# Out projection of a hybrid decoder layer: the first two groups of output columns contract over seven row blocks, and over the eighth when both are through

## The chip, the cores and the metric

One core of a Trainium2 chip runs the whole program. The metric is the device time of one execution in microseconds (us); a kernel's time is the median of several runs. A profiled execution also has a span, from its first instruction to its last. The engines are called PE (TensorE, the matrix unit; PEld is its weight load), DVE (VectorE), ACT (ScalarE), POOL (GpSimd) and SP (SyncE, which issues most transfers).

## What is computed

A decoder layer over 512 tokens of width 1024 in float32. Two token mixers run side by side, a dilated attention and a state-space layer; their merged result passes the out projection and is added to the input; a SwiGLU network, a gated embedding and a norm follow.

```python
h = h + (gate_attn * attn_d + gate_ssm * ssm_d) @ w_out      # the out projection, 1024 x 1024
n2 = rmsnorm(h, g_ffn)
h = h + (silu(n2 @ w_ffn_gate) * (n2 @ w_ffn_up)) @ w_ffn_down
h = h + sigmoid(h @ w_ple_gate) * (p @ w_ple_proj)
return rmsnorm(h, g_final)
```

## The kernel before

Activations lie transposed: 128 features on the partitions, 512 tokens along the row, and a width of 1024 is eight such row blocks. Every float32 matrix product is made of three passes. An operand is split into a high part (rounded to the format that PE multiplies fast) and a low part (the rest), and `mm3` issues high x high (L407), high weights x low activations (L408) and low weights x high activations (L409) into one PSUM bank. `gemm` does this for each row block of the contraction, so one group of 128 output columns over eight row blocks is 24 matmuls of 512 columns.

The weights of a group come as one chunk of 128 x 1024. SP loads it into a `raw` buffer (four of them); ACT rounds it to `whi`; DVE subtracts to get `wlo` (three buffers of each, in turn). `gemm` asks for the split of the next chunks at its fourth row block (`ws.ahead(2)`). The high part is put on ACT's queue at once. The low part is deferred, and is put on DVE's queue when the program's own estimate of time says that `whi` is there:

```python
sca.copy(hi[:, :sz], t[:, :sz])
def low():
    dve.tensor_sub(lo[:, :sz], t[:, :sz], hi[:, :sz].bitcast(F32))
    while self.nd < min(i + 1 + RAW_BUFS, len(chunks)):
        self.dma()
defer(dve, low, hi)
```

The engines run their queues in the order in which this program is written and estimated; an instruction that waits holds everything behind it on its engine.

The merge loop ends with the eighth row block of the merged activation `mT`: DVE makes the sum `t1`, ACT rounds it into `mT[:, 0, 7]`, and DVE subtracts for the low part `mT[:, 1, 7]`. Then the out projection goes over its eight groups m = 0 to 7. For each: four transposes of the input on PE (L403) into an `aux` bank and a copy of it to `h1T` on ACT; 24 matmuls of `mT` with the chunk `wo` into an `mm` bank; an add of the bank to `h1T` on DVE (the add); a scaled rounding to `h1g` on ACT (the scaling); a `SCALAR_TENSOR_TENSOR` on DVE for the low part of `h1g`; and on POOL the square of `h1T` and its sum in `ssq`. `h1g` is what the SwiGLU network reads. The wrappers record every DVE, ACT and POOL operation at L167.

Of the kernel before, what the change touches and what calls it, by code (L numbers as in the profile page):

```python
# [20 lines left out]
KD = D // P  # L21
# [58 lines left out]
def kernel(  # L80
# [15 lines left out]
    def tile_name(ap):  # L96
        return getattr(ap, "tensor", ap).name
# [107 lines left out]
    def nm(s):  # L205
        uid[0] += 1
        return f"{s}_{uid[0]}"
# [4 lines left out]
    def bank(tag):  # L212
        name = nm(tag)
        used = banks[tag]
        if len(used) >= 4:
            bank_free[name] = last_read.get(used[-4], 0.0)
        used.append(name)
        return psum.tile([P, 512], F32, tag=tag, name=name, bufs=4)

    def mm_ps():  # L220
        return bank("mm")

    def aux_ps():
        return bank("aux")
# [13 lines left out]
    class Weights:  # L238
# [40 lines left out]
        def get(self, key, more=1):  # L279
            i = self.np  # L280
            self.np += 1
            assert keys[i] == key, (keys[i], key)
            self.ahead(more)
            wh, wl = self.hl.pop(i)
            if tile_name(wl) not in ready:
                flush(True)
            return wh, wl
# [61 lines left out]
    get = ws.get  # L349
# [7 lines left out]
    def flush(force=False):  # L357
        for item in list(held):
            eng, aps, fn = item
            if force or when(*aps) <= max(now(), eng.free):  # L360
                held.remove(item)
                fn()
# [9 lines left out]
    def tick(limit=3.0, kinds=KINDS, keys=()):  # L372
        flush()
        for item in [item for item in bg if item[2] in kinds]:
            while item[0] <= now() and dve.lag() < limit and sca.lag() < limit:
                if keys and done.issuperset(keys):
                    return
                try:
                    item[0] = next(item[1]) + now()
                except StopIteration:  # L380
                    bg.remove(item)
                    break
# [18 lines left out]
    def transpose(ps, src, n=P):  # L401
        pe_step(ps, 0.07, src)
        nc.tensor.transpose(ps, src, ident[:n, :n])  # L403

    def mm3(ps, lh, ll, rh, rl, start, stop):
        pe_step(ps, 3 * (0.0135 + 0.000417 * rh.free_size()), lh, ll, rh, rl)
        nc.tensor.matmul(ps, lhsT=lh, rhs=rh, start=start, stop=False)  # L407
        nc.tensor.matmul(ps, lhsT=lh, rhs=rl, start=False, stop=False)  # L408
        nc.tensor.matmul(ps, lhsT=ll, rhs=rh, start=False, stop=stop)  # L409

    def gemm(ps, w, c0, act, start=True, stop=True, k0=0):
        wh, wl = w
        ah, al = act
        nk = wh.shape[1]
        for k in range(nk):
            mm3(ps, wh[:, k, c0:c0 + P], wl[:, k, c0:c0 + P], ah[:, k0 + k, :], al[:, k0 + k, :],
                start and k == 0, stop and k == nk - 1)
            if k == 3:
                ws.ahead(2)
            if k < nk - 1:  # L420
                tick()
# [827 lines left out]
    ps = mm_ps()  # L1249
# [75 lines left out]
    ps = aux_ps()  # L1325
# [84 lines left out]
    mT = apool.tile([P, 2, KD, T], F32R, tag="A", name="mT")  # L1410
    flush(True)
    for mp in range(4):
# [10 lines left out]
        for j in range(2):  # L1423
            m = 2 * mp + j
# [25 lines left out]
    for r in range(4):  # L1450
        pt = L4.tile([P, PLE], F32, tag="pt", name=nm("pt"), bufs=4)
        pool.dma_start(pt, p_r[r])
        pts.append(pt)
    for m in range(KD):
        ps = aux_ps()
        for r in range(4):
            transpose(ps[:, r * P:(r + 1) * P], xr[:, r, m * P:(m + 1) * P])
        sca.copy(h1T[:, m], ps)
        ps = mm_ps()
        gemm(ps, get("wo"), 0, (mT[:, 0], mT[:, 1]))  # L1460
        dve.tensor_add(h1T[:, m], h1T[:, m], ps)
        sca.activation(h1g[:, 0, m], h1T[:, m], AF.Copy, scale=gffn[:, m:m + 1])
        dve.scalar_tensor_tensor(h1g[:, 1, m], h1T[:, m], gffn[:, m:m + 1],
                                       h1g[:, 0, m].bitcast(F32), op0=ALU.mult, op1=ALU.subtract)
        if m == 0:
            pool.tensor_mul(ssq, h1T[:, m], h1T[:, m])
        else:
            sq = L4.tile([P, T], F32, tag="sq", name=nm("sq"), bufs=2)
            pool.tensor_mul(sq, h1T[:, m], h1T[:, m])
            pool.tensor_add(ssq, ssq, sq)  # L1470
# [25 lines left out]
    for hf in range(2):  # L1496
        for f in range(NF):
# [16 lines left out]
            if hf == 1 and 3 <= f < 7:  # L1514
                r = f - 3
                ps = aux_ps()
# [6 lines left out]
        if hf == 1:  # L1523
            late = L4.tile([P, 2, 4, D], F32, tag="B", name="late")
            h3, proj = late[:, 0], late[:, 1]
            for c in range(2):
                wph, wpl = get("pp")
                cs = slice(512 * c, 512 * c + 512)
                for r in range(4):
                    sl = slice(r * P, (r + 1) * P)  # L1530
                    ps = aux_ps()
# [3 lines left out]
        for m in range(KD):  # L1535
            ps = mm_ps()
# [53 lines left out]
    for kh in range(4):  # L1590
        w = get("pg")
# [54 lines left out]
    for r in range(4):  # L1646
        for c0, n in ((512, 512),) if r < 3 else ((512, 256), (768, 256)):
            pt_ = aux_ps()[:, 0:n]
            back(pt_, c0 // P, n // P, r)
            ps = mm_ps()[:, 0:n]  # L1650
# [53 lines left out]
```

## Time and profile before

| what | value |
|---|---|
| time, median of 3 runs | 936.71 us (936.27 to 937.2) |
| the profiled execution's own time | 936.02 us |
| its span | 934.2 us |
| PE busy | 922.1 us, 99% of the span |
| DVE, ACT, POOL busy | 492.7, 354.4, 128.9 us |
| granted clock of PE, mean | 0.996 |

A granted clock of 1.00 is 2.4 GHz and 0.50 is 1.2 GHz. A start time in a row counts from the beginning of the span. A row's duration of a matmul is longer than its distance to the next, since they overlap; the distance is what it costs.

### The profile page before, as it was taken

What the parts mean: (1) busy time and instruction counts of PE and PEld (TensorE: products, weight loads), DVE (VectorE), ACT (ScalarE), POOL (GpSimd) and SP (SyncE); (2) the same over time, 40 slices, a digit from 0 to 9 for tenths busy, and PEclk for the clock granted to TensorE, in tenths of its full rate; (3) what the DMA queues carried; (4) which work ended last, traced back from release to release, by engine and by line L of the source; (5) the groups of instructions that cost most, each with busy time, mean ns of one, the idle gap of its engine ahead of it and who ended that gap; (6) DMA issues with size and microseconds to landing.
All of it is one profiled execution on the core that took longest, in us unless ns stands there. A gap on an engine that the chain in (4) does not pass through costs nothing.

```text
span 934.2 us, 11591 instructions
## 1 busy us (share of the span) xinstructions
PE 922.1 (99%) x4539; PEld 776.9 (83%) x4539; DVE 492.7 (53%) x795; ACT 354.4 (38%) x514; POOL 128.9 (14%) x211
## 2 busy tenths in 40 slices
PE   9999999999999999999999999999999999999995
PEld 8888888888988888888788888888888888888885
DVE  6973685577675573356655443432243443234536
ACT  5434555445453543322432322322223332332423
POOL 4117960000000000000143111110001111100021
PEclk9999999999999999999999999999999999999998
DMA  8629314225243542322333333223333333133402
GB/s 242 204 89 157 117 46 116 79 80 116 69 116 88 148 129 77 105 91 77 124 116 91 101 103 91 76 62 110 113 113 91 100 103 98 50 93 99 158 1 91
DMA packets 165103, 96.33 MB, mean 103 GB/s; under 512 B 19985, under 2 KB 158009, under 8 KB 164921
## 3 DMA queue, kind: packets, MB, share of 16 engines
q1 hardware_dynamic: 162936, 92.68, 35.5%
q10 hardware_dynamic: 1520, 1.64, 0.6%
q0 software_dynamic: 592, 1.28, 0.4%
q8 instruction: 35, 0.57, 0.2%
q14 instruction: 20, 0.16, 0.1%
HBM read 90.84 MB, written 4.75 MB: 102 GB/s over the span
## 4 chain that ended last, share of the span: by engine, by line
PE 95%; DVE 2%; DMA 1%; ACT 1%; issue 0%; SPq 0%; DVEq 0%; ACTq 0%
PE mm L408 22%; PE mm L409 22%; PE mm L407 22%; PE aux L399 6%; PE aux L409 6%; PE aux L407 6%; PE aux L408 6%; PE aux L403 2%; PE mm L1241 1%; DMA raw<-in_w_in_dram 1%; DVE t L167 1%; DVE wlo L167 0%; DVE fst L167 0%; ACT qk L167 0%; DVE pk L167 0%
## 5 line engine op out<-in xcount | busy, mean ns | idle before, releaser
L167 DVE TENSOR_TENSOR wlo<-raw,whi 128x1024 fp32r<-128x1024 f32 (+2 forms) x162 | 192.5, 1201 | 101.2 <-ACT whi L167 96.7
L167 ACT CAST whi<-raw 128x1024 fp32r<-128x1024 f32 (+2 forms) x162 | 160.7, 996 | 126.6 <-issue 57.7
L407 PE MATMUL mm<-xn,whi 128*128 128x512 f32 x352 | 139.3, 396 | 0.0
L409 PE MATMUL mm<-xn,wlo 128*128 128x512 f32 x352 | 137.2, 390 | 0.0
L408 PE MATMUL mm<-xn,whi 128*128 128x512 f32 x352 | 137.1, 390 | 0.0
L409 PEld LDWEIGHTS mm<-xn,wlo 128*128 128x128 f32 x352 | 66.1, 188 | 13.9
L407 PEld LDWEIGHTS mm<-xn,whi 128*128 128x128 f32 x352 | 66.2, 188 | 13.1 <-issue 0.2
L408 PEld LDWEIGHTS mm<-xn,whi 128*128 128x128 f32 x352 | 66.2, 188 | 12.9
L407 PE MATMUL mm<-h1g,whi 128*128 128x512 f32 x176 | 68.9, 392 | 0.0
L407 PE MATMUL aux<-h1g,whi 128*128 128x512 f32 x176 | 68.6, 390 | 0.0
L409 PE MATMUL mm<-h1g,wlo 128*128 128x512 f32 x176 | 68.5, 389 | 0.0
L408 PE MATMUL mm<-h1g,whi 128*128 128x512 f32 x176 | 68.5, 389 | 0.0
L409 PE MATMUL aux<-h1g,wlo 128*128 128x512 f32 x176 | 68.5, 389 | 0.0
L408 PE MATMUL aux<-h1g,whi 128*128 128x512 f32 x176 | 68.5, 389 | 0.0
L407 PE MATMUL mm<-act,whi 128*128 128x512 f32 x176 | 68.5, 389 | 0.0
L408 PE MATMUL mm<-act,whi 128*128 128x512 f32 x176 | 68.5, 389 | 0.0
L409 PE MATMUL mm<-act,wlo 128*128 128x512 f32 x176 | 68.5, 389 | 0.0
L167 POOL TENSOR_TENSOR tg<-tg,tu 128x512 f32<-128x512 f32 x22 | 28.4, 1291 | 271.9 <-DVE tu L167 260.5
L167 DVE TENSOR_TENSOR h1T<-h1T,mm 128x512 f32<-128x512 f32 x24 | 16.5, 688 | 78.8 <-PE mm L409 78.8
L167 ACT CAST act<-tg 128x512 fp32r<-128x512 f32 x22 | 13.7, 622 | 90.7 <-POOL tg L167 90.7
L1447 POOL DMA_DIRECT2D gfin<-in_g_final_dram x1 | 0.6, 629 | 331.1 <-DVE mT L167 331.1
L167 DVE TENSOR_TENSOR tu<-aux,rs 128x512 f32<-128x512 f32 x22 | 15.2, 691 | 57.4 <-PE aux L409 57.4
(277 smaller groups left out, 1706.5 us busy)
## 6 DMA issues: line engine op xcount, KB each, us to landing
raw<-in_w_in_dram SPq DMA_DIRECT2D x56, 512.0 KB, 3.8
raw<-in_w_ffn_gate_dram SPq DMA_DIRECT2D x22, 512.0 KB, 3.6
raw<-in_w_ffn_up_dram SPq DMA_DIRECT2D x22, 512.0 KB
raw<-in_w_ffn_down_dram SPq DMA_DIRECT2D x16, 384.0 KB, 3.6
raw<-in_w_ffn_down_dram SPq DMA_DIRECT2D x16, 320.0 KB
raw<-in_w_out_dram SPq DMA_DIRECT2D x8, 512.0 KB, 4.4
raw<-in_w_ple_gate_dram SPq DMA_DIRECT2D x8, 512.0 KB, 4.2
Bp<-ks SPq DMA_DIRECT2D x4, 512.0 KB
```

Source lines behind the costliest of these rows:

```text
L167: return fn(dst, *args, **kw)
L399: nc.tensor.matmul(ps, lhsT=lhsT, rhs=rhs, start=start, stop=stop)
L403: nc.tensor.transpose(ps, src, ident[:n, :n])
L407: nc.tensor.matmul(ps, lhsT=lh, rhs=rh, start=start, stop=False)
L408: nc.tensor.matmul(ps, lhsT=lh, rhs=rl, start=False, stop=False)
L409: nc.tensor.matmul(ps, lhsT=ll, rhs=rh, start=False, stop=stop)
L1241: nc.tensor.matmul(o, lhsT=a[:, k, sl], rhs=wv0[kh][w][:, k % 4], start=first and k == 0, stop=r % 2 == 1 and kh == 1 and part == 2 and k ...
L1447: pool.dma_start(gfin, g_final.partition_broadcast(P))
```

## The change

The transposes and the copy become a function `back_x`. Groups 0 and 1 are first taken over row blocks 0 to 6 and left open in their two banks; their eighth row blocks follow, that of group 0 and then that of group 1, as steps of the loop over m, each with its add, scaling and the rest behind it. Groups 2 to 7 are as before.

```diff
-    for m in range(KD):
+    def back_x(m):
         ps = aux_ps()
         for r in range(4):
             transpose(ps[:, r * P:(r + 1) * P], xr[:, r, m * P:(m + 1) * P])
         sca.copy(h1T[:, m], ps)
+
+
+    first = []
+    for m in range(2):
+        back_x(m)
+        w = get("wo")
         ps = mm_ps()
-        gemm(ps, get("wo"), 0, (mT[:, 0], mT[:, 1]))
+        gemm(ps, tuple(a[:, 0:KD - 1] for a in w), 0, (mT[:, 0], mT[:, 1]), stop=False)
+        first.append((ps, w))
+    for m in range(KD):
+        if m < 2:
+            ps, w = first[m]
+            gemm(ps, tuple(a[:, KD - 1:KD] for a in w), 0, (mT[:, 0], mT[:, 1]), start=False, k0=KD - 1)
+        else:
+            back_x(m)
+            ps = mm_ps()
+            gemm(ps, get("wo"), 0, (mT[:, 0], mT[:, 1]))
         dve.tensor_add(h1T[:, m], h1T[:, m], ps)
         sca.activation(h1g[:, 0, m], h1T[:, m], AF.Copy, scale=gffn[:, m:m + 1])
```

What stands on the queues shows more than the diff. On PE, before, group 0 (bank mm_3967) ends with its seventh and eighth row blocks, each waiting for ACT and DVE, and group 1 (bank mm_4005) follows:

```order
L409 MATMUL mm_3967<-mT,wlo_3868 128x512
L407 MATMUL mm_3967<-mT,whi_3867 128x512 [waits Activation_49]
L408 MATMUL mm_3967<-mT,whi_3867 128x512 [waits DVE_49]
L409 MATMUL mm_3967<-mT,wlo_3868 128x512
L403 MATMUL aux_3999<-cst,xr 128x128 x4
L407 MATMUL mm_4005<-mT,whi_3902 128x512
```

With the change, PE comes to the eighth row blocks of group 0 (mm_3967) and group 1 (mm_3998) one behind the other, after the first seven of both, and then to group 2 (mm_4045, weights whi_3980 and wlo_3981):

```order
L407 MATMUL mm_3967<-mT,whi_3867 128x512 [waits Activation_49]
L408 MATMUL mm_3967<-mT,whi_3867 128x512 [waits DVE_49]
L409 MATMUL mm_3967<-mT,wlo_3868 128x512
L407 MATMUL mm_3998<-mT,whi_3902 128x512
L408 MATMUL mm_3998<-mT,whi_3902 128x512
L409 MATMUL mm_3998<-mT,wlo_3903 128x512
L403 MATMUL aux_4039<-cst,xr 128x128 x4
L407 MATMUL mm_4045<-mT,whi_3980 128x512 [waits Activation_49]
L408 MATMUL mm_4045<-mT,whi_3980 128x512
L409 MATMUL mm_4045<-mT,wlo_3981 128x512 [waits DVE_49]
```

The wait on the eighth row block stands 25 PE instructions later than before: four transposes and group 1's first 21 matmuls have moved ahead of it.

On DVE the place is the start of the out projection, from the add of group 0 on; the lines with + are of the changed kernel, and wlo_3981 is the low part of group 2's weights:

```order
 L167 TENSOR_TENSOR h1T<-h1T,mm_3967 128x512
 L167 SCALAR_TENSOR_TENSOR h1g<-h1T,gffn,h1g 128x512
+L167 TENSOR_TENSOR h1T<-h1T,mm_3998 128x512
+L167 SCALAR_TENSOR_TENSOR h1g<-h1T,gffn,h1g 128x512
 L167 TENSOR_TENSOR wlo_3981<-raw_3803,whi_3980 128x1024
-L167 TENSOR_TENSOR wlo_4022<-raw_3877,whi_4021 128x1024
-L167 TENSOR_TENSOR h1T<-h1T,mm_4005 128x512
-L167 SCALAR_TENSOR_TENSOR h1g<-h1T,gffn,h1g 128x512
+L167 TENSOR_TENSOR wlo_4012<-raw_3877,whi_4011 128x1024
```

The subtraction for group 2's low weights stood behind group 0's add and low part alone; now it stands behind those of groups 0 and 1.

On ACT the place is the same. Before (whi_3980 and whi_4021 are the high weights of groups 2 and 3):

```order
L167 CAST whi_3980<-raw_3803 128x1024 [waits DMAHW3_49]
L167 ACTIVATE h1g<-h1T,gffn 128x512 [waits DVE_49]
L167 COPY h1T<-aux_3999 128x512 [waits PE_49]
L167 CAST whi_4021<-raw_3877 128x1024 [waits DMAHW4_49]
L167 ACTIVATE h1g<-h1T,gffn 128x512 [waits DVE_49]
```

and with the change (whi_4011 are group 3's):

```order
L167 CAST whi_3980<-raw_3803 128x1024 [waits DMAHW3_49]
L167 COPY h1T<-aux_3992 128x512 [waits PE_49]
L167 CAST whi_4011<-raw_3877 128x1024 [waits DMAHW4_49,PE_49]
L167 ACTIVATE h1g<-h1T,gffn 128x512 [waits DVE_49] x2
L167 COPY h1T<-aux_4039 128x512 [waits PE_49]
```

Both scalings moved behind the rounding of group 3's weights, and that rounding now waits for PE: it writes the buffer of whi_3867, which PE reads until group 0's eighth row block.

## Rows read from the trace of the kernel before

**Rows 1.** The page: the span, and busy time and share of each engine.

```profile
span 934.2 us, 11591 instructions
PE 922.1 (99%) x4539; PEld 776.9 (83%) x4539; DVE 492.7 (53%) x795; ACT 354.4 (38%) x514; POOL 128.9 (14%) x211
```

**Rows 2.** Waits of PE: line, releaser, us in total, times, longest.

```profile
PE mm L408 <- DVE mT L167: 0.2, 1, 0.2
PE mm L407 <- ACT mT L167: 0.2, 1, 0.2
```

**Rows 3.** Timeline of PE, group 0's end: start, duration, instruction, idle before and releaser.

```profile
460.73 0.39 PE L409 MATMUL mm<-mT,wlo 128*128 128x512 f32 x1
461.29 0.50 PE L407 MATMUL mm<-mT,whi 128*128 128x512 f32 x1 [0.17 <-ACT mT L167]
462.01 0.50 PE L408 MATMUL mm<-mT,whi 128*128 128x512 f32 x1 [0.22 <-DVE mT L167]
462.35 0.40 PE L409 MATMUL mm<-mT,wlo 128*128 128x512 f32 x1
...
462.94 0.48 PE L407 MATMUL mm<-mT,whi 128*128 128x512 f32 x1
```

**Rows 4.** Timeline of PE, end of group 1 and start of group 2.

```profile
468.05 0.39 PE L408 MATMUL mm<-mT,whi 128*128 128x512 f32 x1
468.28 0.39 PE L409 MATMUL mm<-mT,wlo 128*128 128x512 f32 x1
...
468.87 0.48 PE L407 MATMUL mm<-mT,whi 128*128 128x512 f32 x1
469.18 0.39 PE L408 MATMUL mm<-mT,whi 128*128 128x512 f32 x1
469.41 0.40 PE L409 MATMUL mm<-mT,wlo 128*128 128x512 f32 x1
```

**Rows 5.** Timeline of DVE, 448 to 512 us.

```profile
461.27 0.69 DVE L167 TENSOR_TENSOR mT<-t,mT 128x512 fp32r<-128x512 f32 x1 [0.69 <-ACT mT L167]
...
464.33 0.75 DVE L167 SCALAR_TENSOR_TENSOR h1g<-h1T,gffn,h1g 128x512 fp32r<-128x512 f32 x1 [0.79 <-ACT h1g L167]
...
468.71 0.69 DVE L167 TENSOR_TENSOR h1T<-h1T,mm 128x512 f32<-128x512 f32 x1
470.19 0.88 DVE L167 SCALAR_TENSOR_TENSOR h1g<-h1T,gffn,h1g 128x512 fp32r<-128x512 f32 x1 [0.79 <-ACT h1g L167]
471.61 1.69 DVE L167 TENSOR_TENSOR wlo<-raw,whi 128x1024 fp32r<-128x1024 f32 x1 [0.55 <-ACT whi L167]
```

**Rows 6.** Timeline of ACT, 448 to 512 us.

```profile
450.30 1.05 ACT L167 CAST whi<-raw 128x1024 fp32r<-128x1024 f32 x1 [3.48 <-issue]
...
462.53 1.05 ACT L167 CAST whi<-raw 128x1024 fp32r<-128x1024 f32 x1
...
469.43 0.72 ACT L167 ACTIVATE h1g<-h1T,gffn 128x512 fp32r<-128x512 f32 x1 [3.71 <-DVE h1T L167]
```

**Rows 7.** Timeline of PE, last use of the buffer that the cast at 450.30 overwrites.

```profile
449.83 0.39 PE L408 MATMUL aux<-yt,whi 128*128 128x512 f32 x1
```

**Rows 8.** Timeline of POOL, 448 to 512 us.

```profile
465.49 1.06 POOL L167 TENSOR_TENSOR ssq<-h1T 128x512 f32<-128x512 f32 x1
...
470.60 1.62 POOL L167 TENSOR_TENSOR ssq<-ssq,sq 128x512 f32<-128x512 f32 x1
```

**Rows 9.** Timeline of all engines, 456 to 466 us: two weight subtractions of DVE.

```profile
456.71 1.22 DVE L167 TENSOR_TENSOR wlo<-raw,whi 128x1024 fp32r<-128x1024 f32 x1
...
465.00 2.64 DVE L167 TENSOR_TENSOR wlo<-raw,whi 128x1024 fp32r<-128x1024 f32 x1
```

**Rows 10.** Timeline of PE: the last matmul of the program.

```profile
924.09 0.28 PE L409 MATMUL mm<-whi,h 128*128 128x256 f32 x1
```

**Rows 11.** Windows behind it: busy by engine, then PEclk, DMA share, GB/s.

```profile
924.50:926.50 2.00, 0.00 (x0) 0.00 (x0) 1.72 (x9) 1.98 (x4) 0.00 (x0) 1.00 0.02 4
926.50:927.00 0.50, 0.00 (x0) 0.00 (x0) 0.47 (x4) 0.49 (x3) 0.00 (x0) 0.61 0.00 0
927.00:930.00 3.00, 0.00 (x0) 0.00 (x0) 2.72 (x11) 0.75 (x3) 0.00 (x0) 0.50 0.24 92
```

## The prediction

> **What bounds the kernel now.** I read the page first, for the bound, then the waits of PE, then the timelines of PE, DVE, ACT and POOL around the start of the out projection, and last the granted clock behind the last matmul. PE is busy for 922.1 of 934.2 us [rows 1], so what the change is worth is the time by which PE gets through sooner or later; the other engines count only where PE waits for them. At the out projection PE waits twice, for the high and for the low part of the last row block of mT [rows 2]. Those rows say 0.2 us each, but a matmul's end is modelled there; the distance of starts says more. Group 0's seventh row block ends with the start at 460.73. At the usual distance of 0.23 (468.05 to 468.28) [rows 4] the three matmuls of the eighth would start at 460.96, 461.18 and 461.41; they start at 461.29, 462.01 and 462.35 [rows 3]. So the whole stall is 462.35 - 461.41 = 0.94 us. It ends when DVE has subtracted the low part, 461.27 + 0.69 = 461.96 [rows 5], 0.05 before PE's 462.01.
>
> **What the change removes.** The eighth row block now comes 25 PE instructions later: after the end at 460.73 come four transposes (0.59 us from the last matmul before them to the first behind, 462.35 to 462.94 [rows 3]) and 21 matmuls of 0.23 us, some 5.4 us in all. The low part is there at 461.96, so the stall goes entirely: -0.94 us. The number of matmuls, transposes and PSUM adds is the same; PE's work costs nothing more, since the three passes just go to another bank, as they do at every group's border. All of PE's starts up to group 2 are then 0.94 earlier: the last matmul of both groups at 468.28 - 0.94 = 467.34 [rows 4], group 0's own last one three distances ahead of that, at 466.66, and group 2's first three at 467.93, 468.24 and 468.47.
>
> **What the change adds.** The third matmul of group 2 (L409) needs wlo of that group. Its raw weights and its high part are long there: the cast starts at 462.53 [rows 6]. Its low part is late, because DVE's queue is strict. Before, that subtraction stood behind group 0's add and low part of h1g and ran while PE was busy with group 1. Now it stands behind the adds and low parts of both groups, and these can't begin before PE is through with both eighth row blocks. On DVE, behind the waiting adds, are queued the low weights of groups 2, 3 and 4; PE waits for the first of these. The chain, step by step:
>
> - Add of group 0: a group's last matmul at 468.28 was followed by its add at 468.71 [rows 4, 5], so 0.43 later; 466.66 + 0.43 = 467.09, and with 0.69 it ends at 467.78.
> - Scaling of group 0 on ACT. It stands behind the cast of group 3's weights, which waits until PE has read group 0's high weights for the last time, with L408 at 466.43. A cast with the same kind of wait came 0.47 behind such a matmul (449.83 to 450.30) and took 1.05 [rows 6, 7]: 466.90 to 467.95. The scaling takes 0.72 [rows 6]: 467.95 to 468.67. This queueing costs 0.13 against a start right behind the add.
> - Low part of h1g for group 0: 0.04 later (469.43 + 0.72 to 470.19 [rows 5, 6]), 0.75 to 0.88 us long [rows 5]: 468.71 to about 469.5.
> - Add of group 1, long ready: 0.69, to 470.2. Scaling 0.03 behind it, 0.72: to 470.95. Low part of group 1, 0.04 behind: 470.99 to 471.87.
> - Low weights of group 2. Alone this takes 1.22 (at 456.71); at 465.00 it took 2.64, with POOL's ssq running from 465.49 to 466.55 in it; at 471.61 it took 1.69 [rows 5, 8, 9]. There POOL's sum, put in at 470.60 while DVE was at a low part of h1g, ended at 472.22, and the subtraction 1.08 after that, at 473.30, which is 3.11 behind the start of the low part (470.19) [rows 5, 8]. The rows look as if the two engines took turns here. The new order repeats this pattern, with POOL's sum put in while DVE is at the low part of group 1, so I take the 3.11: 470.99 + 3.11 = 474.10. Bounds: 471.87 + 1.22 = 473.09 if DVE goes first, less 0.13 if a low part runs at its shorter 0.75, and 471.87 + 2.64 = 474.51.
> - PE behind it: 0.05 as at 461.96, and 0.11 because the distance to the next matmul was 0.34 instead of 0.23 after that wait (462.01 to 462.35) [rows 3]. So group 2 goes on as if its third matmul had started at 474.26.
>
> Before, that matmul started at 469.41 [rows 4]. The net of stall removed and stall added is 474.26 - 469.41 = **+4.85 us**, between +3.7 (472.96 + 0.16) and +5.3 (474.51 + 0.16).
>
> Later steps: the low weights of group 3 follow at once on DVE (1.2, to 475.3), and PE wants them 24 matmuls and four transposes later, near 480, so this is one stall and not a train. The loads that SP issues when a raw buffer comes free (groups 6 and 7) start some 6 us later, and are wanted four groups, over 20 us, later. POOL's sum of squares ends as late as group 7's add does, as before. PE is 99% busy to the end [rows 1] and has no other wait in which the delay could vanish, so it stays.
>
> **The clock.** PE would sit idle from 468.63 (468.24 and 0.39 for that matmul) to 474.15, 5.5 us. The only such idle time in this trace is behind the last matmul, which ends at 924.37 [rows 10]: the granted clock was 1.00 (2.4 GHz) up to 926.50, 0.61 on the mean in the next half microsecond, so that it fell some 0.11 into it, and 0.50 (1.2 GHz) after [rows 11]. The fall came 2.2 us after the work ended, and 5.5 is far longer; I expect the same fall in the middle of the out projection. No row shows how long the lower level holds once work is back. At it, a matmul of 512 columns takes twice the distance, so half of that time is lost. As bounds I take nothing (back at once) and a low level as long as the idle itself, half of 5.5, 2.75 us; I take the middle, **+1.4 us**, as no row is nearer to either end.
>
> The Trainium skill ("TensorE: Matmul & The Clock Gate", section "Why this matters for your kernels") speaks against such a gap: idle time between bursts of matmuls brings the lower rate, and busy time is needed to leave it. By the row alone a return at once is open, and the sum could be 4.85; by the rule the cost is above nothing, and the sum is nearer to the 6.25 below.
>
> **The sum.** -0.94 is inside the 4.85; 4.85 + 1.4 = +6.25 us. On the profiled execution: 936.02 + 6.25 = 942.27 us. That execution lies 0.69 below the median of the runs shown, 936.71, and within 0.3 us of the lowest; the forecast for the median is 936.71 + 6.25 = **942.96**, 943.0.
>
> **Rivals.**
>
> *The stall without the clock.* The level holds, or returns at once: 936.71 + 4.85 = 941.6 us (940.4 to 942.0 by the bounds of the chain). For it: no row shows the level fall in a gap between two stretches of work, nor a matmul at it. Against it: the fall after 2.2 us [rows 10, 11].
>
> *Not slower: PE finds group 2's low weights ready.* Then only the removed stall counts, 936.71 - 0.94 = 935.8 us, which is within 0.2%. That needs DVE to make them before the two adds. The point from which it decides is 468.47: at that time PE wants them, and if DVE had ended them by then nothing would wait; an end up to 469.36 would still cost no more than was won. DVE is free from 461.96 to 467.09, so there would be time enough; against it stands the order of its queue, in which every DVE row of the trace stands in sequence.
>
> *A short chain.* If DVE and ACT overlapped more than I read (an add that starts at 466.9, no queue behind the cast, no turn for POOL), the chain would still have two adds, two scalings, two low parts and one subtraction: 2 x 0.69 + 2 x 0.72 + 2 x 0.75 + 1.22 = 5.5 us behind 467.09, so 472.6, and +3.3 us, 940.0. It can't fall within 0.2%.
>
> *A long stay at the lower clock,* beyond the 2.75: over 945 us. Nothing in the trace speaks for it, and nothing excludes it.
>
> **Chances.** Stall with a clock loss up to the bound 0.62; stall without it 0.27; a chain still shorter 0.03; a longer stay 0.04; no stall 0.04. The range: from 936.71 + 3.7 = 940.4 to 936.71 + 5.3 + 2.75 = 944.8, and half a microsecond more on each side for the spread of the runs (936.27 to 937.2): 939.9 to 945.3. A change of 0.2%, 1.9 us, is about what a measurement of this kernel can tell from none. Faster by more than that would need twice the stall that is there: 0.01. Within it: the case without a stall, 0.04. Slower: 0.95.
>
> **What would show it.** In the profile of the changed kernel: no wait of L407 or L408 on mT; group 0's last matmul near 466.7; on ACT the cast of group 3's weights at 466.9 and two scalings behind it; on DVE add, low part, add, low part, subtraction, with the last ending near 474.1; one wait of PE at L409 on DVE's wlo of over 5 us; and a granted clock below 1.00 in the microseconds from 471 on, with matmuls at twice the distance for a while after 474. If that subtraction ends near 473.1, DVE went before POOL; if no clock below 1.00 shows, the second term falls. Wrong as a whole it would be if PE's third matmul of group 2 started before 470, or if a wait downstream took the delay up.

## The result

The changed kernel takes 943.49 us (median of 6 runs, 943.05 to 944.66) against 936.68 us (6 runs, 936.27 to 937.33): a ratio of 1.0074, 95% interval 1.0064 to 1.0084. It is slower by 6.8 us, where 6.25 were forecast, at 943.49 in a range of 939.9 to 945.3.

The page of the changed kernel, span and busy time by engine, against [rows 1]:

```profile
span 941.7 us, 11591 instructions
PE 924.2 (98%) x4539; PEld 779.0 (83%) x4539; DVE 491.7 (52%) x795; ACT 354.6 (38%) x514; POOL 128.2 (14%) x211
```

The number of instructions is the same and PE's busy time has grown by 2.1 us; the rest of the 7.5 us of span is idle. Not all of it is the change's: 1.14 us lies ahead of the out projection (below). The waits of PE show where the rest is. The two rows on mT [rows 2] are gone, and the first row is new (so is one of 0.2 us on `xu`, which lies in the first 30 us, ahead of the change):

```profile
PE mm L409 <- DVE wlo L167: 5.4, 1, 5.4
```

The timeline of PE in the changed kernel shows the same places as [rows 3, 4]: the end of group 0's seventh row block, the start of group 1, the last matmul of both groups, the start of group 2, and the start of group 3 at the end.

```profile
461.87 0.39 PE L409 MATMUL mm<-mT,wlo 128*128 128x512 f32 x1
...
462.46 0.48 PE L407 MATMUL mm<-mT,whi 128*128 128x512 f32 x1
...
468.48 0.39 PE L409 MATMUL mm<-mT,wlo 128*128 128x512 f32 x1
...
469.06 0.48 PE L407 MATMUL mm<-mT,whi 128*128 128x512 f32 x1
469.38 0.40 PE L408 MATMUL mm<-mT,whi 128*128 128x512 f32 x1
475.18 0.79 PE L409 MATMUL mm<-mT,wlo 128*128 128x512 f32 x1 [5.40 <-DVE wlo L167]
475.77 0.63 PE L407 MATMUL mm<-mT,whi 128*128 128x512 f32 x1
476.20 0.63 PE L408 MATMUL mm<-mT,whi 128*128 128x512 f32 x1
...
482.27 0.48 PE L407 MATMUL mm<-mT,whi 128*128 128x512 f32 x1
```

This execution came to the out projection 1.14 us later than the one of before (DVE's low part of mT starts at 462.41 instead of 461.27), with the same program up to there; so stage times are counted from that instruction. In the kernel before, group 3 starts 13.52 us after it:

```profile
474.79 0.48 PE L407 MATMUL mm<-mT,whi 128*128 128x512 f32 x1
```

In the changed kernel it is 482.27 - 462.41 = 19.86, so +6.34 us by the end of group 2. From there to the last matmul of the program both need the same: 931.59 - 482.27 = 449.32, and 924.09 - 474.79 = 449.30. Nothing was given back and nothing lost later. The same holds for the seven runs below: there this distance is 449.31 or 449.32.

The chain of the work that ended last, in the changed kernel, in order of time (start, us, what), runs through just what the forecast listed:

```profile
467.74 0.24 PE mm L408
467.98 0.02 issue
468.00 1.06 ACT whi L167
469.06 0.69 ACT h1g L167
469.75 0.02 issue
469.78 0.88 DVE h1g L167
470.65 0.61 DVE h1T L167
471.26 0.02 issue
471.29 0.73 ACT h1g L167
472.02 0.03 issue
472.04 0.04 DVE h1g L167
472.08 0.76 issue
472.84 2.29 DVE wlo L167
475.14 0.04 issue
475.18 0.79 PE mm L409
```

It begins at the matmul that lets ACT cast group 3's weights, goes over both scalings and the two adds' low parts, and ends with the low weights that PE waits for. And the clock: the windows of the changed kernel around the wait (length, busy by engine, then the granted clock):

```profile
469.50:471.50 2.00, 0.28 (x2) 0.00 (x0) 1.47 (x2) 0.46 (x2) 0.78 (x2) 1.00 0.00 0
471.50:472.00 0.50, 0.00 (x0) 0.00 (x0) 0.00 (x0) 0.50 (x2) 0.50 (x1) 0.79 0.00 0
472.00:475.00 3.00, 0.00 (x0) 0.00 (x0) 2.96 (x2) 1.42 (x3) 1.97 (x2) 0.50 0.00 0
475.00:478.00 3.00, 2.82 (x7) 2.24 (x8) 2.39 (x3) 0.00 (x0) 0.00 (x0) 0.50 0.51 142
478.00:479.00 1.00, 1.00 (x5) 0.82 (x4) 0.00 (x0) 0.00 (x0) 0.00 (x0) 0.69 0.91 260
```

PE ends its work at 469.78, the level falls from 1.00 (2.4 GHz) to 0.50 (1.2 GHz) some 2.0 us later, and it is still low when PE works again, up to about 478.6. In that stretch the matmuls start 0.43 us apart (475.77 to 476.20) instead of 0.23. So the level costs half of the time for which PE works at it: it starts again at 475.18, the mean of 0.69 in the last window puts the rise at 478.62, and half of these 3.4 us is 1.7.

### The profile page after: what moved, and what is told of

It reads as the page before. It is cut to its first block, busy times and chain, and to the rows that moved or that the text cites. A ratio compares the mean times of both kernels' runs of the same rounds, so it can differ in the third digit from the quotient of the medians.

```text
span 941.7 us, 11591 instructions
## 1 busy us (share of the span) xinstructions
PE 924.2 (98%) x4539; PEld 779.0 (83%) x4539; DVE 491.7 (52%) x795; ACT 354.6 (38%) x514; POOL 128.2 (14%) x211
## 4 chain that ended last, share of the span: by engine, by line
PE 96%; DVE 2%; ACT 1%; DMA 0%; issue 0%; ACTq 0%; DVEq 0%
PE mm L409 22%; PE mm L407 22%; PE mm L408 22%; PE aux L409 6%; PE aux L408 6%; PE aux L407 6%; PE aux L399 6%; PE aux L403 3%; PE mm L1241 1%; DVE wlo L167 0%; DMA cst<-in_consts_dram 0%; DVE fst L167 0%; PE warm L441 0%; ACT qk L167 0%; DVE pk L167 0%
```

## The experiments

The theory: PE loses time only because the subtraction for group 2's low weights stands behind two adds that wait for PE, and then because the clock falls in the gap; POOL's sum makes the subtraction longer. The rivals: that contracting two groups in pieces costs by itself, that the clock costs nothing, that DVE's subtraction did not wait for POOL. Runs that were made together share their runs of the kernel before (936.74 us in the first set of four, 936.62 us in the second of three).

### The subtraction ahead of the adds

In the changed kernel the deferred subtraction is put on DVE's queue when group 0's first part has been issued:

```diff
         first.append((ps, w))
+        if m == 0:
+            flush(True)
```

> The changed kernel with one difference: the subtraction for group 2's low weights is put on DVE's queue when group 0's first seven row blocks have been issued, ahead of the two adds. If the whole loss comes from where that subtraction stood, PE waits neither on mT nor on these weights, and the time is that of before less the stall taken away, 936.7 - 0.94 = 935.7 us; group 3's low weights are still behind both adds and should end some 0.3 us before PE wants them. If contracting the two groups in pieces (two open banks, the adds close together) costs by itself, the time stays above that of before: over 936.7, up to 943 if the order on DVE has nothing to do with it.

Measured: 935.75 us, ratio 0.9991 (0.9983 to 1.0). PE waits neither on mT nor on weights. DVE's timeline shows the subtraction at work where DVE was idle before, and the add behind it on time:

```profile
461.92 0.69 DVE L167 TENSOR_TENSOR mT<-t,mT 128x512 fp32r<-128x512 f32 x1 [0.69 <-ACT mT L167]
464.27 1.22 DVE L167 TENSOR_TENSOR wlo<-raw,whi 128x1024 fp32r<-128x1024 f32 x1 [1.66 <-ACT whi L167]
467.74 0.69 DVE L167 TENSOR_TENSOR h1T<-h1T,mm 128x512 f32<-128x512 f32 x1 [2.24 <-PE mm L409]
```

PE comes to group 3 with

```profile
474.49 0.48 PE L407 MATMUL mm<-mT,whi 128*128 128x512 f32 x1
```

which is 12.57 us after the low part of mT (474.49 - 461.92), 0.95 sooner than before: the whole stall of 0.94 is won. So the pieces cost nothing that shows, and one place in a queue turns a loss of 6.8 us into a time 1.0 below that of before. That gain is read from the stage; the interval of the ratio reaches no change.

### The late subtraction without the change

The kernel before, with the subtractions for groups 2 and 3 held until both adds and low parts are on DVE's queue:

```diff
-            defer(dve, low, hi)
+            if i - keys.index("wo") in (2, 3):
+                kept.append(low)
+            else:
+                defer(dve, low, hi)
...
+        if m == 1:
+            for fn in kept:
+                fn()
```

> The kernel before, its PE order untouched (groups 0 and 1 whole, with the stall on mT), with one difference: the subtractions for group 2's and group 3's low weights are held until behind the adds and low parts of groups 0 and 1 on DVE. If their place on DVE is what costs, the loss comes without the change: group 1's add at 468.7, its low part at 470.2, the subtraction's end near 473.3, PE's third matmul of group 2 at 473.4 instead of 469.4, so 4.0 us, and with an idle gap of 3.8 us a fall of the clock and some 1.7 us more: 942.4 us. If the pieces cost, this kernel stays at 936.7.

Measured: 942.82 us, ratio 1.0067 (1.0053 to 1.008). The waits of PE (its lines are numbered four higher in this kernel) have the stall on mT as before and the new one:

```profile
PE mm L413 <- DVE wlo L167: 3.8, 1, 3.8
...
PE mm L412 <- DVE mT L167: 0.2, 1, 0.2
PE mm L411 <- ACT mT L167: 0.2, 1, 0.2
```

The third matmul of group 2 and the first of group 3:

```profile
474.02 0.67 PE L413 MATMUL mm<-mT,wlo 128*128 128x512 f32 x1 [3.81 <-DVE wlo L167]
...
481.09 0.48 PE L411 MATMUL mm<-mT,whi 128*128 128x512 f32 x1
```

Here DVE's low part of mT starts at 461.88, so the first of the two is 4.00 us later in the stage than before, as expected, and group 3 5.69. So the loss needs no regrouping of matmuls, only that order on DVE.

### The gap filled with work

The changed kernel with 22 matmuls that nobody reads, between group 2's transposes and its first matmul:

```diff
             back_x(m)
+            if m == 2:
+                fill = aux_ps()
+                for i in range(22):
+                    nc.tensor.matmul(fill, lhsT=mT[:, 0, i % KD, 0:P], rhs=mT[:, 0, i % KD], start=True, stop=True)
```

> The changed kernel with 22 more matmuls of 512 columns on PE, into a bank that nobody reads, between group 2's transposes and its first matmul: some 5.0 us of work in a gap of 5.4 us. DVE, ACT and POOL have the same order. If the lower granted clock after the gap is what costs beyond the wait, the clock stays at 1.00, PE's third matmul of group 2 starts as late as before, and the time is 1.7 us below the changed kernel, 941.8 us, though PE does more. If the clock costs nothing and the wait is all of it, the time stays at 943.5 or rises by what sticks out of the gap.

Measured: 940.97 us, ratio 1.0045 (1.003 to 1.006), 2.5 us below the changed kernel's 943.49 with 22 matmuls more. The timeline of PE and two windows:

```profile
468.23 5.27 PE L1477 MATMUL aux<-mT 128*128 128x512 f32 x22
...
474.37 0.50 PE L409 MATMUL mm<-mT,wlo 128*128 128x512 f32 x1 [0.42 <-DVE wlo L167]
474.70 0.40 PE L407 MATMUL mm<-mT,whi 128*128 128x512 f32 x1
...
479.84 0.48 PE L407 MATMUL mm<-mT,whi 128*128 128x512 f32 x1
```

```profile
468.00:474.00 6.00, 5.94 (x29) 4.63 (x27) 4.42 (x5) 3.06 (x5) 3.69 (x3) 1.00 0.02 3
474.00:476.00 2.00, 1.64 (x7) 1.38 (x8) 2.00 (x3) 0.00 (x0) 0.00 (x0) 1.00 0.22 49
```

DVE's low part of mT starts at 461.59 here. The third matmul of group 2 comes as late as in the changed kernel (12.78 us after it, there 12.77), but the clock stays at 1.00 and group 3 starts 4.73 us later than before instead of 6.34. The wait and the clock are two separate costs. By the stage the clock's is 1.6 us; the rest of the 2.5 between the medians no row of the stage shows.

### Half of the gap filled

The same with 11 matmuls (`range(11)`).

> As the run with 22 matmuls in the gap, with 11: 2.5 us of work and some 2.9 us idle. The end of the wait is the same in both. If only an idle time of several microseconds brings the lower clock, the time is that of the filled gap, 941.0 us; if 2.9 us idle are enough, it is that of the changed kernel, 943.4. Behind the last matmul of the kernel before the fall came after 2.2 us, so I expect a fall, and 942 to 943.4.

Measured: 943.17 us (941.02 to 943.76 in 4 runs), ratio 1.0061 (1.0046 to 1.0077). The wait is 2.89 us, and in the profiled execution the clock falls in it all the same; two matmuls and the windows:

```profile
474.15 0.80 PE L409 MATMUL mm<-mT,wlo 128*128 128x512 f32 x1 [2.89 <-DVE wlo L167]
...
482.45 0.48 PE L407 MATMUL mm<-mT,whi 128*128 128x512 f32 x1
```

```profile
471.50:473.00 1.50, 0.00 (x0) 0.00 (x0) 1.50 (x2) 0.90 (x1) 1.50 (x1) 1.00 0.00 0
473.00:473.50 0.50, 0.00 (x0) 0.00 (x0) 0.50 (x1) 0.00 (x0) 0.01 (x1) 0.85 0.00 0
473.50:474.00 0.50, 0.00 (x0) 0.00 (x0) 0.50 (x1) 0.00 (x0) 0.00 (x0) 0.50 0.00 0
474.00:480.00 6.00, 5.85 (x14) 4.65 (x15) 2.37 (x3) 0.00 (x0) 0.00 (x0) 0.50 0.73 209
480.00:481.00 1.00, 1.00 (x6) 0.81 (x5) 0.00 (x0) 0.00 (x0) 0.00 (x0) 0.91 0.86 260
```

PE works for six microseconds at 0.50 (474.15 to 480.18, by the mean of 0.91 in the last window), longer than in the changed kernel with its longer gap, and with DVE's low part of mT at 461.38 group 3 starts 7.55 us later than before. The spread of its runs, 2.7 us, says that other executions lost less. The lowest, 941.02, is that of the filled gap, and its mean granted clock is too: 0.997 over the whole execution, against 0.992 in the profiled one. So in that execution the same wait seems to have passed without a fall; no profile of it shows this.

### POOL's sum out of the way

Two tries. In the first, POOL's square and sum for group 1 were only written behind group 2's add:

```diff
-        else:
-            sq = L4.tile([P, T], F32, tag="sq", name=nm("sq"), bufs=2)
-            pool.tensor_mul(sq, h1T[:, m], h1T[:, m])
-            pool.tensor_add(ssq, ssq, sq)
+        elif m > 1:
+            for n in (1, 2) if m == 2 else (m,):
+                sq = L4.tile([P, T], F32, tag="sq", name=nm("sq"), bufs=2)
+                pool.tensor_mul(sq, h1T[:, n], h1T[:, n])
+                pool.tensor_add(ssq, ssq, sq)
```

> The changed kernel with POOL's square and sum for group 1 put behind group 2's add, so that POOL has nothing to do while DVE makes group 2's low weights. If DVE's subtraction waited for its turn behind POOL's sum, it takes 1.2 us instead of 2.3, group 1's low part 0.75 instead of 0.88, and PE goes on 1.1 us sooner: a wait of 4.3 us instead of 5.4, the clock still falls, 942.4 us. If the two don't take turns, the subtraction ends as late as in the changed kernel and the time is 943.5.

Measured: 943.38 us, ratio 1.0071 (1.0057 to 1.0085), and it tells nothing on the question: POOL had no waiting work ahead of them, so they ran as early as ever:

```profile
470.82 1.04 POOL L167 TENSOR_TENSOR sq<-h1T 128x512 f32<-128x512 f32 x1 [1.23 <-DVE h1T L167]
471.94 1.59 POOL L167 TENSOR_TENSOR ssq<-ssq,sq 128x512 f32<-128x512 f32 x1
```

In the second, group 2's square and sum come first on POOL's queue, `for n in (2, 1)`, wait for group 2's add, and hold group 1's behind them.

> As the run with POOL's square and sum for group 1 later, where they ran as early as ever, since nothing that POOL waits for stood ahead of them. Here those of group 2 stand ahead, so POOL can't begin before group 2's add. If DVE's subtraction waits for its turn behind POOL's sum, it takes 1.2 us instead of 2.3 and group 1's low part 0.75 instead of 0.88; PE's wait is 4.3 us instead of 5.4, the clock still falls in it or behind it, and the time is 1.1 us below the changed kernel, 942.3 us. If the two don't take turns, the rows and the time stay: 943.4.

Measured: 941.78 us (941.7 to 944.24 in 4 runs), ratio 1.006 (1.0047 to 1.0074). DVE at group 1's low part and group 2's subtraction, and PE's wait:

```profile
471.00 0.75 DVE L167 SCALAR_TENSOR_TENSOR h1g<-h1T,gffn,h1g 128x512 fp32r<-128x512 f32 x1 [0.79 <-ACT h1g L167]
471.67 1.22 DVE L167 TENSOR_TENSOR wlo<-raw,whi 128x1024 fp32r<-128x1024 f32 x1
```

```profile
PE mm L409 <- DVE wlo L167: 4.2, 1, 4.2
```

The subtraction takes 1.22 us instead of 2.28 and the low part 0.75 instead of 0.88; PE's wait is 1.2 us shorter. POOL's sum in DVE's way was 1.2 of the 5.4 us.

### Group 3's subtraction sooner as well

On top of the first experiment, a second flush right behind group 0's add:

```diff
         dve.tensor_add(h1T[:, m], h1T[:, m], ps)
+        if m == 0:
+            flush(True)
```

> As the run with group 2's subtraction ahead of the adds, and group 3's right behind group 0's add instead of behind both adds and low parts. There group 3's ended 0.45 us before PE wanted it, so it cost nothing; here it ends some 3 us earlier. If that reading is right, the time is the same, 935.7 us, 0.9 below that of before; if a wait on group 3's weights was hidden in it, the time falls further, below 935.3.

Measured: 935.65 us, ratio 0.999 (0.9981 to 0.9999). It is the same time as with group 2's alone, so in the first experiment group 3's low weights, still behind both adds, were in time. These two versions are the fastest of all, each about 1 us below the kernel before: within the 0.2% that I called hard to tell, with intervals that just reach or exclude no change.

## Why the prediction was right, step by step

**The stall removed, -0.94 us.** Right: no wait on mT is left, and with the second loss taken away the gain is 0.95 by the stage and 1.0 by the medians.

**The stall added.** Right step by step. Less the 1.14 us of offset, the changed kernel has group 0's add at 467.16 (467.09 forecast), the cast of group 3's weights at 466.86 (466.90), the first scaling at 467.88 (467.95), group 1's scaling at 470.15 (470.23), its low part at 470.90 (470.99), and the end of the subtraction at 475.13 - 1.14 = 473.99 (474.10). PE's third matmul of group 2 starts 4.63 us later in the stage than before; 4.85 was forecast, with 0.11 of it for a slower pick-up that is counted with the clock here, so 4.74 against 4.63.

**Who goes first, DVE or POOL.** Right: POOL. The lower bound of the chain, DVE alone at 1.22 us and the shorter low part, is what the second of the POOL experiments measured: there the subtraction ends at 472.89, less 0.10 of offset 472.79, where 472.96 was the bound.

**The clock, +1.4 us between 0 and 2.75.** Right in kind; the size was a guess in the middle of two bounds, and that 1.4 came near the changed kernel's 1.71 is luck. By rows: group 3's delay less that of the third matmul is 6.34 - 4.63 = 1.71 us in the changed kernel, 0.09 with the gap filled (4.73 - 4.64), 1.69 with the late subtraction alone (5.69 - 4.00), 1.44 and 2.25 in the two POOL experiments (6.06 - 4.62, 5.68 - 3.43), and 2.92 with the gap half filled (7.55 - 4.63). So this term is not one number. That half of the low time is lost was right: PE worked at 0.50 for 3.4 us in the changed kernel and for 6.0 with the gap half filled, and half of that is 1.7 and 3.0. How long that time is was the open point, and it varies: with the late subtraction alone the executions of 943.2 and 943.68 us have a mean granted clock of 0.992, those of 942.34 and 942.45 us 0.995. The upper bound tied the low stretch to the length of the gap, half of 5.5 us; the half-filled gap shows that this tie is wrong, since a gap of 2.89 us cost 2.92, which belongs to the rival of a longer stay. The Trainium skill's rule ("TensorE: Matmul & The Clock Gate", section "Why this matters for your kernels") that idle gaps between bursts bring the lower rate agrees with the profiled executions: five gaps of 2.9 to 5.4 us brought 0.50, one of 0.4 us did not.

**The sum.** 6.25 forecast; 6.34 in the profiled execution's stage, 6.81 between the medians. The half microsecond between these two stays open. It is of the size by which the clock's term varies, but the mean granted clocks of the changed kernel's six executions, 0.992 to 0.994, lie on both sides of the profiled one's 0.993. It is also of the size by which the way to the out projection varies: the offset that is 1.14 us in the changed kernel's profile is 0.05 to 0.65 in those of the experiments.

**The rivals.** Without a clock loss: 941.6 was forecast, and 940.97 was measured when the gap was filled. Not slower, 935.8: it needed DVE to make the weights ahead of the adds; the changed kernel doesn't, and when it is made to, it takes 935.75. A short chain, +3.3 us: no, the changed kernel's is 4.63; it is 3.43 only with POOL out of the way.

## What to carry to other kernels

When an instruction moves back on one engine, whatever needs its result begins later on another engine, and so does everything that stands behind that on the other engine's queue. So when work is moved on one engine to hide a wait, read the queues of the others and ask what stands behind the instructions that now begin later, and who waits for that. Here a 0.94 us stall was removed and a 5.4 us one made, by work (the next weights) that had nothing to do with the wait and could run in DVE's five idle microseconds, as the first experiment shows. A stall of a few microseconds on PE can cost more than itself, since the clock falls and PE then works at half speed for some time (here 1.4 to 2.9 us more, in five profiles with stalls of 2.9 to 5.4 us); filling the gap with dead matmuls takes that part away, the right order takes away all.

## What was not expected of the hardware

The lower clock does not end with the idle time and is not in proportion to it. It came some 2.0 us after the last matmul in the changed kernel, but in the run with the late subtraction alone the clock fell only when PE was already at work again: 1.00 up to 474.00 and 0.60 on the mean in the next microsecond, with the first matmul after the wait at 474.02. With POOL's sum only written later, the idle time began at 469.28 and the level was still 1.00 at 474.00. A gap of 2.89 us cost 2.92 us on top of itself in one execution, a gap of 5.40 us only 1.44 in another.

DVE's subtraction of 128 x 1024 took 1.22 us with POOL quiet and 2.28 with POOL's sum put in first; its low part of h1g went from 0.88 to 0.75. And an instruction written later on a queue runs no later if nothing ahead of it waits: POOL's square started 0.07 us after its input's add had ended (470.82, the add from 470.07 for 0.68) although it was written behind a whole group more.
